# Attention branches: the 512-column score tile ahead of the 384-column one, and POOL scaling it by two per-partition numbers

## The chip, the cores and the metric

The kernel runs on one core of one Trainium2 chip. Its engines are PE (matrix products), DVE (vector operations), ACT (activation functions), POOL (GpSimd) and SP (which here issues DMAs). The metric is the device time of one execution in microseconds. Before the change it is 1286.28 us, the median of 3 runs (1286.25 to 1287.93).

## What is computed

A trunk of two layers on a sequence of 512 tokens, all in float32. Each layer has a mixer of three parallel parts (sparse attention, gated linear attention, spatial gating), an output projection and a feed-forward block. The change touches only the attention's two large branches, selected and window attention:

```python
NSA_HEADS, HEAD_DIM, SEQ, DEPTH = 8, 64, 512, 2
def masked_softmax(s, mask):
    s = where(mask, s, -inf)
    e = exp(s - max(s))
    return e / sum(e)
p = masked_softmax(einsum('bqghd,bgqmd->bghqm', qb, ksel), tok <= t)
o_slc = einsum('bghqm,bgqmd->bqghd', p, vsel)
p = masked_softmax(einsum('bqghd,bkgd->bghqk', qb, kwb), wmask)
o_win = einsum('bghqk,bkgd->bqghd', p, vwb)
return gb[..., 0:1] * o_cmp + gb[..., 1:2] * o_slc + gb[..., 2:3] * o_win
```

With 512 tokens both branches attend to every earlier token, each with keys and values of its own. Their two gates are per token, head and branch.

## The kernel before, in words

The attention stage of a layer (in `mixer`, from line 1188 on) loops over 8 heads, taken in pairs (`hp`, `hh`), and in each head over 2 branches (`br`). A branch works on 4 query tiles `i` of 128 tokens; tile `i` has 128 x (i+1) key columns, so the score tiles are 128, 256, 384 and 512 columns wide. The two narrow ones (`i` below `NBOTH` = 2) are computed for both branches at once when a head starts (lines 1209 to 1225); the other two in the loop at line 1228, the 384-column one first. For each tile PE multiplies queries by keys into a PSUM bank (L1234, L1235: the second product also adds the causal mask), DVE takes the negated row maximum (L1237), and ACT takes the exponential with the row sums as a by-product (L1239; L1222 for the narrow tiles). A row sum is a column of `den`, which is 128 x 4.

When all four sums are there, DVE takes their reciprocals at once (L1244) and multiplies them by the gates of the four tiles (L1245), giving `rr`. Then every tile is scaled in place by its column of `rr`, on three engines (line 1247): tiles 0 and 1 by DVE (L1253), tile 2 by ACT (L1251), tile 3 by POOL (L1249), where the column is handed over as a second tensor broadcast along the row. A dependency added by hand (line 1255) keeps POOL's scaling behind DVE's last one.

Then come the products with the values. For key tiles `j` in the groups `JG` = (0), (1), (2, 3), PE transposes the 128 x 128 blocks of the scaled tiles into a PSUM bank (L1262; group 0 takes tiles 0, 1, 2, 3 in that order), ACT copies the bank into a high part (L299) and DVE takes the low part (L300, both in `split_psum`), and PE multiplies both parts by the values into the head's output bank (L1275, L1276). The compressed branch is added (L1286, L1287), ACT and DVE bring the result out (L1288, L1289).

Score banks form a ring of 3, transpose banks a ring of 2. A scheduler sets the order on each engine's queue from the program order, priorities and costs of its own; at run time each engine takes its queue in order and waits on semaphores. The scheduler puts other work between: products of the output projection (L336 to L338, their weights cast by ACT at L318 and split by DVE at L321, their sums added by DVE at L500), the preparation of queries (L1120, L1125, L1126; L1186 is a copy of them on POOL) and the compressed branch's softmax (`prep_c`, L1140 to L1160).

Of the kernel before, what the change touches and what calls it, by code (L numbers as in the profile page):

```python
# [16 lines left out]
ALU = mybir.AluOpType  # L17
AX = mybir.AxisListType

P = 128  # L20
# [4 lines left out]
NT = SEQ // P  # L25
# [27 lines left out]
NBOTH = 2  # L53
# [90 lines left out]
def trunk_kernel(ctx: ExitStack, tc: tile.TileContext, a, out):  # L144
# [24 lines left out]
    def small(n, tag, bufs=4, dt=F32):  # L169
        return sm.tile([P, n], dt, tag=tag, name=nm(tag), bufs=bufs)  # L170
# [396 lines left out]
    def mixer(l, norm, xkt, eu=None):  # L567
# [65 lines left out]
        with tc.tile_pool(name=f"mx{l}", bufs=1, reuse_waits="tile") as mp:  # L633
# [427 lines left out]
            with tc.tile_pool(name=f"mt{l}", bufs=1, reuse_waits="tile") as tp_:  # L1061
# [126 lines left out]
                for hp in range(H // 2):  # L1188
                    if hp % 2 == 0:
                        okt[hp // 2] = kt_tile()  # L1190
                    kt = okt[hp // 2]
                    oc = tmp()
                    for hh in range(2):
                        h = 2 * hp + hh
                        g, h4 = h // GH, h % GH
                        prep(h, 0)
                        qa = qm1[h % GH]
                        for n in range(h, h + 2) if h < H - 1 else ():
                            if n == 0 or n > h:
                                load_q(n)  # L1200
                        O = psum(OT[h % len(OT)])
                        first = True
                        for br in range(2):
                            if br == 1:
                                prep(h, 2)
                            if br == 0:
                                dens = [small(NT, "den", 4) for _ in range(2)]
                                both = []
                                for i in range(NBOTH):
                                    n = P * (i + 1)  # L1210
                                    S = psum("s")
                                    S3 = S[:, 0 : 2 * n].rearrange("p (b k) -> p b k", b=2)
                                    tk = slice(i * P, (i + 1) * P)
                                    kd = km1[g][:, :, 0:2, :] if i else km1[g][:, :, 6, :]
                                    nc.tensor.matmul(S3, qst[g][:, h4, tk], km2[g][:, :, 0:n], start=True, stop=False)
                                    nc.tensor.matmul(S3, qa[:, tk], kd, start=False, stop=True)
                                    nmx = small(2, "nmx", 8)
                                    nc.vector.tensor_reduce(nmx, S3, axis=AX.X, op=ALU.max, negate=True)
                                    pb = []
                                    for b_ in range(2):  # L1220
                                        p_ = tp_.tile([P, n], F32, tag=f"P{i}", name=nm("P"), bufs=P0B[i])
                                        nc.scalar.activation(p_, S3[:, b_], AF.Exp, bias=nmx[:, b_ : b_ + 1],  # L1222
                                                             accum_out=dens[b_][:, i : i + 1])
                                        pb.append(p_)
                                    both.append(pb)
                            den = dens[br]
                            ps_ = [pb[br] for pb in both]
                            for i in range(NBOTH, NT):
                                n = P * (i + 1)
                                S = psum("s")  # L1230
                                tk = slice(i * P, (i + 1) * P)
                                kd = km1[g][:, br, 0:6, :]
                                kd = kd.rearrange("p (n s) c -> p n s c", s=2)[:, :, 0, :] if i == 2 else kd.rearrange("p (o x) c -> p o x c", o=2)[:, :, 0:3:2, :]
                                nc.tensor.matmul(S[:, 0:n], qst[g][:, h4, tk], km2[g][:, br, 0:n], start=True, stop=False)  # L1234
                                nc.tensor.matmul(S[:, 0:n], qa[:, tk], kd, start=False, stop=True)  # L1235
                                nmx = small(1, "nmx", 8)
                                nc.vector.tensor_reduce(nmx, S[:, 0:n], axis=AX.X, op=ALU.max, negate=True)  # L1237
                                p_ = tp_.tile([P, n], F32, tag=f"P{i}", name=nm("P"), bufs=P0B[i])
                                nc.scalar.activation(p_, S[:, 0:n], AF.Exp, bias=nmx, accum_out=den[:, i : i + 1])  # L1239
                                ps_.append(p_)  # L1240
                            if br == 0:
                                prep(h, 1)
                            rr = small(NT, "rr", 4)
                            nc.vector.reciprocal(rr, den)  # L1244
                            nc.vector.tensor_tensor(rr, rr, gates[:, :, 3 * h + 1 + br], op=ALU.mult)  # L1245
                            scaled = None
                            for i in SORD:
                                if i in ISP:
                                    p3 = nc.gpsimd.tensor_tensor(ps_[i], ps_[i], rr[:, i : i + 1].to_broadcast([P, P * (i + 1)]), op=ALU.mult)  # L1249
                                elif i in ISA:  # L1250
                                    nc.scalar.activation(ps_[i], ps_[i], AF.Copy, scale=rr[:, i : i + 1])  # L1251
                                else:
                                    scaled = nc.vector.tensor_scalar(ps_[i], ps_[i], rr[:, i : i + 1], None, op0=ALU.mult)  # L1253

                            tc.add_manual_dep(p3.ins, scaled.ins.name, mybir.DependencyInfo(mybir.DependencyClass.Sync, mybir.DependencyReason.DATA),
                                              reason="port")
                            for js in JG:
                                T = psum(TT[js[0]])
                                c = 0
                                for j in js:  # L1260
                                    for i in range(j, NT):
                                        nc.tensor.transpose(T[:, c : c + P], ps_[i][:, j * P : (j + 1) * P], ident)  # L1262
                                        c += P
                                if js[0] < JS:
                                    pt = mp.tile([P, 2, c], F32R, tag="PT", name=nm("PT"), bufs=3)
                                    split_psum(pt[:, 0, :], pt[:, 1, :], T[:, 0:c])
                                else:
                                    pf = mp.tile([P, c], F32, tag="PT", name=nm("PT"), bufs=3)
                                    nc.scalar.copy(pf, T[:, 0:c])
                                c = 0  # L1270
                                for j in js:
                                    n = SEQ - j * P
                                    lhs = vst[:, j, br, g].rearrange("p s d -> p (s d)")
                                    if js[0] < JS:
                                        nc.tensor.matmul(O[:, j * P : SEQ], lhs, pt[:, 0, c : c + n], start=first, stop=False)  # L1275
                                        nc.tensor.matmul(O[:, j * P : SEQ], lhs, pt[:, 1, c : c + n], start=False, stop=False)  # L1276
                                    else:
                                        nc.tensor.matmul(O[:, j * P : SEQ], lhs.bitcast(F32), pf[:, c : c + n],
                                                         start=False, stop=False)
                                    first = False  # L1280
                                    c += n
                        prep(h, 3)
                        lhs = vcb[:, g, h4].rearrange("p s d -> p (s d)")
                        hs = slice(64 * hh, 64 * hh + 64)
                        ls = slice(64 - 64 * hh, 128 - 64 * hh)
                        nc.tensor.matmul(O, lhs, pcT[g][0], start=False, stop=False)  # L1286
                        nc.tensor.matmul(O, lhs, pcT[g][1], start=False, stop=True)  # L1287
                        nc.scalar.copy(oc[hs, :], O[ls, :])  # L1288
                        nc.vector.tensor_tensor(oc[hs, :], oc[hs, :], O[hs, :], op=ALU.add)  # L1289
                    split_psum(kt[:, hp % 2, 0, :], kt[:, hp % 2, 1, :], oc)  # L1290
# [416 lines left out]
```

## Time and profile before

| what | value |
|---|---|
| median of 3 runs | 1286.28 us |
| the profiled execution, its own time | 1286.52 us |
| its span in the trace | 1284.7 us |
| outside the span | 1.8 us |
| PE busy | 1257.3 us |
| DVE busy | 918.2 us |
| ACT busy | 677.0 us |
| POOL busy | 160.5 us |
| granted TensorE clock, mean | 0.997 |

The span runs from the first to the last instruction of the trace. In a timeline a row gives the start and duration in us, the engine, the source line, the operation and its tiles (written ones left of the arrow), and in square brackets the idle time just before it and what ended that. Groups give the count, the busy time, the mean in ns of one, and the idle time before them by what ended it. In the view of one line the three numbers behind the count are the shortest, median and longest duration in ns.

### The profile page before, as it was taken

Reading aid. Unit: us, or ns where it says so; the run is one execution under the profiler, and the core shown is the slowest. Engines: PE = TensorE matmul, PEld = TensorE weight load, DVE = VectorE, ACT = ScalarE, POOL = GpSimd, SP = SyncE. Lnnn points to the kernel's source line nnn. Section 1 sums busy time; section 2 is a strip of 40 time slices with the busy share of each in tenths; the row PEclk is TensorE's granted clock in tenths of the full one; section 3 lists DMA queues with packets and bytes.
Section 4 is the critical chain, followed back from the end, with each engine's and each line's share of the span. In section 5 each row is a group of like instructions: output and inputs, shape, how many; then the busy total and the mean of one; then the engine's idle time right before and its main releaser. Section 6 shows DMA issues by size and latency. Waiting matters only on the chain. (4 is left out here: it accounts for less than half of the span.)

```text
span 1284.7 us, 18046 instructions
## 1 busy us (share of the span) xinstructions
PE 1257.3 (98%) x6678; PEld 1038.5 (81%) x6678; DVE 918.2 (71%) x1645; ACT 677.0 (53%) x1288; POOL 160.5 (12%) x157
## 2 busy tenths in 40 slices
PE   8999999999999999999999999999999999999997
PEld 7888788778888888888888877777788888888886
DVE  6767799977856775587446678998767457827775
ACT  6675367864533553354346733788544445515532
POOL 0101222122000100010301012121210001000102
PEclk9999999999999999999999999999999999999999
DMA  6451441034335885483434317210533448754811
GB/s 231 142 180 34 115 108 33 17 87 127 98 105 141 197 232 146 111 200 99 115 94 149 116 34 175 64 33 3 146 98 99 131 117 210 216 130 133 227 66 66
DMA packets 134204, 155.01 MB, mean 121 GB/s; under 512 B 9307, under 2 KB 86885, under 8 KB 134117
## 3 DMA queue, kind: packets, MB, share of 16 engines
q1 hardware_dynamic: 117392, 128.81, 33.3%
q0 software_dynamic: 10208, 20.84, 9.2%
q10 hardware_dynamic: 6516, 4.22, 1.5%
q8 instruction: 52, 0.85, 0.3%
q14 instruction: 36, 0.29, 0.1%
HBM read 149.92 MB, written 2.10 MB: 118 GB/s over the span
## 5 line engine op out<-in xcount | busy, mean ns | idle before, releaser
L318 ACT CAST hl<-raw 128x1024 fp32r<-128x1024 f32 (+3 forms) x170 | 175.2, 1035 | 226.5 <-PE banks L338 160.9
L321 DVE TENSOR_TENSOR hl<-raw,hl 128x1024 fp32r<-128x1024 f32 (+3 forms) x170 | 207.1, 1222 | 94.6 <-ACT hl L318 93.0
L336 PE MATMUL banks<-hl,kt 128*128 128x512 f32 (+2 forms) x688 | 257.9, 375 | 1.1 <-ACT hl L318 1.1
L337 PE MATMUL banks<-hl,kt 128*128 128x512 f32 (+2 forms) x688 | 256.4, 373 | 0.0
L338 PE MATMUL banks<-hl,kt 128*128 128x512 f32 (+2 forms) x688 | 256.1, 373 | 0.0
L337 PE MATMUL banks<-kt,hl 128*128 128x512 f32 x384 | 151.5, 394 | 0.0
L338 PE MATMUL banks<-kt,hl 128*128 128x512 f32 x384 | 151.1, 394 | 0.0
L336 PE MATMUL banks<-kt,hl 128*128 128x512 f32 x384 | 150.4, 394 | 0.0
L336 PEld LDWEIGHTS banks<-hl,kt 128*128 128x128 f32 x688 | 129.5, 188 | 23.6 <-ACT hl L318 1.9
L337 PEld LDWEIGHTS banks<-hl,kt 128*128 128x128 f32 x688 | 129.5, 188 | 21.8 <-DVE hl L321 0.3
L338 PEld LDWEIGHTS banks<-hl,kt 128*128 128x128 f32 x688 | 129.4, 188 | 21.7
L318 ACT CAST hl<-wx 128x1024 fp32r<-128x1024 f32 x48 | 50.5, 1052 | 79.8 <-PE banks L338 69.1
L337 PEld LDWEIGHTS banks<-kt,hl 128*128 128x128 f32 x384 | 72.2, 188 | 14.7 <-DVE kt L295 0.9
L338 PEld LDWEIGHTS banks<-kt,hl 128*128 128x128 f32 x384 | 72.3, 188 | 13.7
L336 PEld LDWEIGHTS banks<-kt,hl 128*128 128x128 f32 x384 | 72.0, 188 | 13.3 <-ACT kt L299 0.3
L321 DVE TENSOR_TENSOR hl<-wx,hl 128x1024 fp32r<-128x1024 f32 x48 | 58.7, 1224 | 18.4 <-ACT hl L318 18.2
L500 DVE TENSOR_TENSOR xT<-xT,banks 128x512 f32<-128x512 f32 x56 | 37.5, 681 | 47.6 <-PE banks L338 47.6
L337 PE MATMUL banks<-act,hl 128*128 128x512 f32 x172 | 67.0, 390 | 0.0
L338 PE MATMUL banks<-act,hl 128*128 128x512 f32 x172 | 66.9, 389 | 0.0
L336 PE MATMUL banks<-act,hl 128*128 128x512 f32 x172 | 66.9, 390 | 0.0
L300 DVE TENSOR_TENSOR PT<-banks,PT 128x384 fp32r<-128x384 f32 (+1 forms) x96 | 54.6, 597 | 14.1 <-ACT PT L299 13.2
L336 PE MATMUL banks<-hl,act 128*128 128x512 f32 (+1 forms) x164 | 63.0, 384 | 0.0
(356 smaller groups left out, 2404.1 us busy)
## 6 DMA issues: line engine op xcount, KB each, us to landing
raw<-in_w_gate_dram SPq DMA_DIRECT2D x44, 512.0 KB, 3.9
raw<-in_w_up_dram SPq DMA_DIRECT2D x44, 512.0 KB, 4.0
raw<-in_w_in_dram SPq DMA_DIRECT2D x32, 512.0 KB, 3.7
raw<-in_w_down_dram SPq DMA_DIRECT2D x36, 256.0 KB, 4.0
raw<-in_w_down_dram SPq DMA_DIRECT2D x18, 512.0 KB, 3.7
raw<-in_w_out_dram SPq DMA_DIRECT2D x16, 512.0 KB, 4.3
raw<-in_cmp_w_k_dram SPq DMA_DIRECT2D x8, 512.0 KB, 3.9
raw<-in_cmp_w_v_dram SPq DMA_DIRECT2D x8, 512.0 KB, 4.9
```

Of the source, the lines that this page charges most:

```text
L300: nc.vector.tensor_tensor(lo, src, hi.bitcast(F32), op=ALU.subtract)
L318: last_cast[:] = [nc.scalar.copy(hl[:, 0, 0:n], raw[:, 0:n])]
L321: e_.tensor_tensor(hl[:, 1, 0:n], raw[:, 0:n], hl[:, 0, 0:n].bitcast(F32), op=ALU.subtract)
L336: nc.tensor.matmul(ps, lh, rh, start=start, stop=False, skip_group_check=skip)
L337: nc.tensor.matmul(ps, lh, rl, start=False, stop=False, skip_group_check=skip)
L338: return nc.tensor.matmul(ps, ll, rh, start=False, stop=stop, skip_group_check=skip)
L500: nc.vector.tensor_tensor(xT[:, m, :], xT[:, m, :], ps, op=ALU.add)
```

## The change

The loop over the two wide tiles runs backwards, so the 512-column tile (`i` = 3) comes before the 384-column one. As soon as the 512-column tile's exponential is there, DVE takes the reciprocal of its one row sum into a new small tile `rc` (L1243 of the changed kernel), and POOL scales the tile by two per-partition numbers, that reciprocal and the gate (L1244). The three other sums are inverted later (L1248), multiplied by their gates (L1249) and used as before (ACT L1255, DVE L1257). The dependency that kept POOL behind DVE is gone. Each of the 32 branches has one DVE instruction more. Lines behind the edit move: the transposes are L1264, the products with the values L1277 and L1278, the scores L1235 and L1236, the maximum L1238, the exponential L1240.

```diff
                             ps_ = [pb[br] for pb in both]
-                            for i in range(NBOTH, NT):
+                            rc = small(NT, "rc", 4)
+                            for i in range(NT - 1, NBOTH - 1, -1):
...
                                 nc.scalar.activation(p_, S[:, 0:n], AF.Exp, bias=nmx, accum_out=den[:, i : i + 1])
-                                ps_.append(p_)
+                                ps_.insert(NBOTH, p_)
+                                if i == NT - 1:
+                                    nc.vector.reciprocal(rc[:, i : i + 1], den[:, i : i + 1])
+                                    nc.gpsimd.tensor_scalar(p_, p_, rc[:, i : i + 1], gates[:, i, 3 * h + 1 + br : 3 * h + 2 + br], op0=ALU.mult, op1=ALU.mult)
                             if br == 0:
                                 prep(h, 1)
                             rr = small(NT, "rr", 4)
-                            nc.vector.reciprocal(rr, den)
-                            nc.vector.tensor_tensor(rr, rr, gates[:, :, 3 * h + 1 + br], op=ALU.mult)
+                            nc.vector.reciprocal(rc[:, 0:3], den[:, 0:3])
+                            nc.vector.tensor_tensor(rr[:, 0:3], rc[:, 0:3], gates[:, 0:3, 3 * h + 1 + br], op=ALU.mult)
                             scaled = None
                             for i in SORD:
                                 if i in ISP:
-                                    p3 = nc.gpsimd.tensor_tensor(ps_[i], ps_[i], rr[:, i : i + 1].to_broadcast([P, P * (i + 1)]), op=ALU.mult)
+                                    continue
...
-                            tc.add_manual_dep(p3.ins, scaled.ins.name, mybir.DependencyInfo(mybir.DependencyClass.Sync, mybir.DependencyReason.DATA),
-                                              reason="port")
```

The scheduler orders the two attention stages anew; outside them the queues keep their order. On DVE, in the first branch of the second head of layer 0, the queue before (`den` holds the row sums, `P` the tiles, `nmx` the maxima, `PT` the low parts of transposed tiles):

```order
L1244 RECIPROCAL rr_2022<-den_1992 128x4
L1237 TENSOR_REDUCE nmx_2058<-banks 128x1
L300 TENSOR_TENSOR PT_1949<-banks,PT_1949 128x512
L300 TENSOR_TENSOR PT_1957<-banks,PT_1957 128x384
L1245 TENSOR_TENSOR rr_2022<-rr_2022,gates_278 128x4
L1237 TENSOR_REDUCE nmx_2064<-banks 128x1
L1253 TENSOR_SCALAR P_1998<-P_1998,rr_2022 128x128
L1253 TENSOR_SCALAR P_2006<-P_2006,rr_2022 128x256
```

And the same branch in the changed kernel:

```order
L1243 RECIPROCAL rc_2014<-den_1996 128x1
L321 TENSOR_TENSOR hl_3066<-raw_3064,hl_3066 128x1024
L300 TENSOR_TENSOR PT_1953<-banks,PT_1953 128x512
L300 TENSOR_TENSOR PT_1961<-banks,PT_1961 128x384
L1248 RECIPROCAL rc_2014<-den_1996 128x3
L1238 TENSOR_REDUCE nmx_2065<-banks 128x1
L1249 TENSOR_TENSOR rr_2029<-rc_2014,gates_278 128x3
L1238 TENSOR_REDUCE nmx_2073<-banks 128x1
L300 TENSOR_TENSOR PT_1969<-banks,PT_1969 128x384
L1257 TENSOR_SCALAR P_2002<-P_2002,rr_2029 128x128
L1257 TENSOR_SCALAR P_2010<-P_2010,rr_2029 128x256
```

The one-column reciprocal, which releases POOL, now stands six rows ahead of the product (L1249) that makes the factors of the other scalings, with a weight split (L321, both operands in SBUF) right behind it.

On PE, where the first branch of layer 0 turns from scores to transposes, the queue before (`hl` are weights of the output projection, `qst` and `qm` queries, `km` keys):

```order
L1234 MATMUL banks<-km_180_1596,qst_1804 128x384
L1235 MATMUL banks<-km_182_1598,qm_184_1600 128x384
L1234 MATMUL banks<-km_180_1596,qst_1804 128x512
L1235 MATMUL banks<-km_182_1598,qm_184_1600 128x512
L336 MATMUL banks<-kt_1591,hl_2898 128x512
L1262 MATMUL banks<-ident,P_1832 128x128
L1262 MATMUL banks<-ident,P_1840 128x128
L1262 MATMUL banks<-ident,P_1848 128x128
```

The transposes of POOL's tile (P_1854) stand three rows further on. And in the changed kernel:

```order
L336 MATMUL banks<-kt_1591,hl_2930 128x512
L1215 MATMUL banks<-km_180_1596,qst_1804 128x256
L1216 MATMUL banks<-km_182_1598,qm_185_1601 128x256
L337 MATMUL banks<-kt_1591,hl_2930 128x512
L338 MATMUL banks<-kt_1591,hl_2930 128x512
L336 MATMUL banks<-kt_1591,hl_2930 128x512
L337 MATMUL banks<-kt_1591,hl_2930 128x512
L338 MATMUL banks<-kt_1591,hl_2930 128x512
L336 MATMUL banks<-kt_680,hl_2930 128x512
L1264 MATMUL banks<-ident,P_1832 128x128
L1215 MATMUL banks<-km_180_1596,qst_1804 128x512
L1264 MATMUL banks<-ident,P_1840 128x128
```

Six products of the output projection and the next head's first scores, which stood behind the first transposes, now stand ahead of them.

## The prediction

> **What bounds the kernel now.** The page comes first. It says which engine is full:
>
> ```profile
> span 1284.7 us, 18046 instructions
> PE 1257.3 (98%) x6678; PEld 1038.5 (81%) x6678; DVE 918.2 (71%) x1645; ACT 677.0 (53%) x1288; POOL 160.5 (12%) x157
> ```
>
> PE is busy 98% of the span, so only places where PE stands still can give time back. The edited lines run in the attention stage alone, from about 176 to 272 us (layer 0) and 807 to 903 us (layer 1). The view by stretches of 10 us (columns: PE, PEld, DVE, ACT, POOL busy us) shows who is full there:
>
> ```profile
> 185.00:195.00 10.00, 9.84 (x53) 7.99 (x52) 9.64 (x23) 8.23 (x24) 1.04 (x1) 1.00 0.01 2
> 225.00:235.00 10.00, 9.15 (x51) 6.81 (x50) 9.91 (x28) 8.21 (x24) 2.08 (x2) 1.00 0.07 21
> 235.00:245.00 10.00, 9.45 (x54) 7.11 (x53) 9.53 (x22) 8.19 (x24) 2.08 (x2) 1.00 0.12 35
> 245.00:255.00 10.00, 9.45 (x54) 7.15 (x53) 7.84 (x21) 9.06 (x27) 2.08 (x2) 1.00 0.00 0
> 255.00:265.00 10.00, 8.75 (x50) 6.64 (x50) 8.95 (x22) 8.39 (x25) 2.08 (x2) 1.00 0.01 2
> 852.00:862.00 10.00, 9.20 (x46) 6.90 (x45) 9.72 (x27) 8.67 (x26) 2.68 (x3) 1.00 0.00 0
> 862.00:872.00 10.00, 9.41 (x57) 7.37 (x56) 9.71 (x23) 8.51 (x24) 1.04 (x1) 1.00 0.19 55
> ```
>
> Three engines are close to full together. PE loses little early, where products of the output projection fill its gaps, and most in the later heads. DVE is at 95% or more while PE has gaps in two stretches of each layer (225 to 245, 852 to 872). Next, the view of the line that is changed, POOL's scaling of the widest tile:
>
> ```profile
> L1249 POOL TENSOR_TENSOR P<-P,rr x32: 1039/1040/1043, 183.3 to 902.0; 128x512 f32<-128x512 f32 x32
>   DVE P L1253: 50.9, 10
> ...
>   PEld banks L1262: 5.3, 12
>   PE banks L1262: 2.3, 8
> ```
>
> It runs 32 times for 1.04 us, often starts when DVE's scaling ends (the 50.9 us of idle POOL cost nothing in themselves), and PE's transposes wait for it: 2.3 us booked on the matmuls, 5.3 us on their weight loads. The timeline of one such place:
>
> ```profile
> 226.44 0.39 PE L336 MATMUL banks<-kt,hl 128*128 128x512 f32 x1
> 226.67 0.40 PE L337 MATMUL banks<-kt,hl 128*128 128x512 f32 x1
> ...
> 227.57 0.17 DVE L1244 RECIPROCAL rr<-den 128x4 f32<-128x4 f32 x1
> ...
> 227.79 1.04 POOL L1249 TENSOR_TENSOR P<-P,rr 128x512 f32<-128x512 f32 x1 [3.19 <-DVE rr L1244]
> ...
> 228.13 0.49 PE L1234 MATMUL banks<-km,qst 128*128 128x512 f32 x1
> 228.23 0.62 DVE L1245 TENSOR_TENSOR rr<-rr,gates 128x4 f32<-128x4 f32 x1
> ...
> 228.89 0.44 PE L1262 MATMUL banks<-ident,P 128*128 128x128 f32 x2 [0.26 <-POOL P L1249]
> ```
>
> A matmul of 512 columns is followed by the next after 0.23 us (226.44 to 226.67). Here 0.76 us pass (228.13 to 228.89), so 0.53 us are lost where 0.26 is booked. The idle time counts from a modelled end and shows about half of the loss.
>
> **The change part by part.** First, POOL's wait. The widest tile is now scored and exponentiated first, its own reciprocal follows at once, and POOL starts without DVE's scalings. What of PE's waits for POOL goes away? At least the booked 2.3 us, at most the 5.3 us of the weight loads (a part of which PE covers by matmuls still streaming). Doubled by the place above, 2.3 becomes 4.6; the middle of the bounds is 3.8. I take 4.0 us for both layers. That the new wait does not come out as late needs rows for what stands between:
>
> ```profile
> L1237 DVE TENSOR_REDUCE nmx<-banks 128x1 f32<-128x512 f32 x16 | 10.9, 681 | 0.0
> L1237 DVE TENSOR_REDUCE nmx<-banks 128x1 f32<-128x384 f32 x16 | 8.8, 547 | 0.8 <-PE banks L1235 0.8
> L1239 ACT ACTIVATE P<-banks,nmx 128x512 f32<-128x512 f32 x16 | 11.2, 700 | 3.0 <-DVE nmx L1237 3.0
> L1239 ACT ACTIVATE P<-banks,nmx 128x384 f32<-128x384 f32 x16 | 9.4, 589 | 2.3 <-PE banks L1262 1.7 <-DVE nmx L1237 0.3 <-DVE PT L300 0.2
> L1239 ACT ACTIVATION_READ_ACCUMULATOR P<-banks,nmx 128x1 f32 x32 | 6.7, 210 | 0.0
> L1244 DVE RECIPROCAL rr<-den x32: 164/174/179, 181.3 to 900.2; 128x4 f32<-128x4 f32 x32
> L1245 DVE TENSOR_TENSOR rr<-rr,gates x32: 93/160/892, 181.9 to 900.4; 128x4 f32<-128x4 f32 x32
> L1245 DVE TENSOR_TENSOR rr<-rr,gates 128x4 f32<-128x4 f32 x32 | 8.6, 268 | 0.3
> L1253 DVE TENSOR_SCALAR P<-P,rr x64: 269/312/355, 182.6 to 901.5; 128x128 f32<-128x128 f32 x32, 128x256 f32<-128x256 f32 x32
> L1186 POOL CAST qm<-qst x12: 602/604/612, 175.1 to 854.4; 64x512 fp32r<-64x512 f32 x12
> L353 POOL TENSOR_TENSOR nacc<-nacc,nsq x21: 1283/1397/1852, 289.0 to 938.8; 128x512 f32<-128x512 f32 x21
> ```
>
> After the widest tile's exponential, ACT still has the 384-column one (0.59 + 0.21 for its sum), then DVE the reciprocal (0.17), the product with the gates (0.16) and two scalings (2 x 0.31): 1.75 us at least, even if nothing stands between. POOL's new instruction with two per-partition scalars isn't in this trace. It reads one wide tile, as the CAST of half the partitions does (0.60 us), and not two, as L353 does (1.40 us); L1249 with its broadcast operand (1.04 us) is nearest, and I take 1.0. All three fit under 1.75 us, so its length costs nothing; beyond 1.75 us each further 0.1 us would cost up to 3.2 us in 32 branches. [...]
>
> Second, DVE. Each branch gets one more reciprocal: 32 x 0.17 = +5.5 us. L1245 is one of two DVE instructions whose operands both lie in SBUF; in the place above it took 0.62 us and ended with POOL's scaling (228.85 and 228.83). Over all 32 it is busy 8.6 us where its median gives 32 x 0.16 = 5.1, so POOL's scaling costs DVE 3.5 us today. With POOL started earlier this is returned where the product stands far enough behind. The order shows that in 20 branches over 1.3 us of other DVE work comes between the one-column reciprocal and the next DVE instruction with two SBUF operands or a scaling. In 8 it follows within 0.8 us, and may be held for 0 to 0.73 us (0.892 less 0.16): 0 to 5.8 us. In 4 more the weight split L321 follows directly:
>
> ```profile
> L321 DVE TENSOR_TENSOR hl<-raw,hl x6: 1215/1222/1752, 169.0 to 231.5; 128x1024 fp32r<-128x1024 f32 x6
> ```
>
> There DVE loses 0 to 0.53 us each (1.752 less 1.222), together 0 to 2.1, or POOL waits 1.2 us, which the 1.75 us hold only in part. DVE's sum: 5.5 - 3.5 + (0 to 7.9) = +2 to +10 us; with something under half of the new holds, +5. How much of that reaches the end? Where DVE is full and PE is not, which is 20 of some 96 us in each layer, about a fifth: +1.0 us. Bounds are 0 and all 10.
>
> Third, edits with one answer. The last tile is now the narrower one, so its reduction and exponential are 0.13 and 0.11 us shorter; in a stage where three engines are nearly full I take nothing for it. The gate multiplication of the widest tile moves into POOL's second scalar, and the product on DVE has three columns, not four: nothing. POOL's queue still holds the query copies (L1186) between scalings; a scaling behind two of them starts up to 1.2 us later. DMA issues keep their order.
>
> Sum against the profiled execution: 1286.52 - 4.0 + 1.0 = 1283.5 us. The median of the runs shown is 0.24 lower (1286.28), so 1283.3 us.
>
> **The rivals.** A measurement here tells a change of about 0.2% (2.6 us) from none: faster means below 1283.7, slower above 1288.9.
>
> *DVE becomes the bound (slower).* The place is the stretch from 245 us on and its twin, where DVE has 1 to 2 us of room in 10. If the holds come at their upper end (+10) and 8 of these 10 us delay the transposed tiles that PE waits for, it is 8 - 4 = +4 us: 1290.3. It decides from a DVE share of 9.5 in 10 in the stretches now at 7.84 and 8.95. The manual wait that the change removes kept POOL's scaling off DVE's, which speaks for it; that 20 of 32 branches have 1.3 us of harmless work between speaks against. [...]
>
> *The wait only changes its name (no change).* ACT's scaling of the 384-column tile already stands idle for the reciprocal's product:
>
> ```profile
> L1251 ACT ACTIVATE P<-P,rr 128x384 f32<-128x384 f32 x32 | 20.0, 624 | 8.3 <-DVE rr L1245 8.3
> ```
>
> That tile is now the last to be exponentiated, and its scaling (0.62 us) the last link before the transposes. If PE then waits for ACT or DVE as long as for POOL, 4.0 come back: 1286.3, give or take 1.5. The same happens if POOL starts no earlier, because the reciprocal stands late in DVE's queue.
>
> *More than the wait goes (faster by more).* PE also waits for the copies of transposed tiles:
>
> ```profile
> L1275 PE MATMUL banks<-PT,vst 128*128 128x512 f32 (+3 forms) x128 | 43.9, 347 | 5.3 <-ACT PT L299 3.2 <-DVE tmp L1289 1.6
> ```
>
> If the full 5.3 us of POOL waits go, and, with transposes grouped earlier, about half of these 3.2: -5.3 - 1.6 = -6.9, 1279.4. Against it: those waits are for ACT's copy, which the change leaves alone.
>
> **How the numbers follow.** The forecast (1281.5 to 1285.0 by itself) gets 0.36: 0.27 of it below 1283.7, 0.09 above. The larger gain gets 0.15, the renamed wait 0.26, the DVE bound 0.23. So faster 0.27 + 0.15 = 0.42, within 0.2% 0.09 + 0.26 = 0.35, slower 0.23. The range 1277.5 to 1290.5 takes in three of the four cases and the DVE case to a little past its middle; outside are about 0.03 below and 0.12 above.
>
> **What would show it.** In the profile after: POOL's scaling as TENSOR_SCALAR of 0.6 to 1.4 us; PE's and PEld's waits for it under 0.5 and 1.5 us together; the product of three columns with a mean of at most 0.25 us; DVE in the stage busier by 2 to 3 us a layer; PE at 9.3 or more in 255 to 265 us. I am wrong if PE still waits for POOL, if L1257 or the product takes 0.8 us in many branches, if waits for ACT's scaling take POOL's place, or if POOL's instruction takes over 1.75 us.

## The result, and the profile after

| | median | runs |
|---|---|---|
| before | 1287.05 us | 6 (1286.25 to 1288.01) |
| after | 1295.08 us | 6 (1294.30 to 1295.74) |
| ratio | 1.0061 | interval 1.0049 to 1.0073 |

The change makes the kernel slower by 8.0 us. The forecast was 1283.3 us with a range of 1277.5 to 1290.5, so both the sign and the range are wrong. The page of the profiled execution (1295.74 us by its own time):

```profile
span 1294.0 us, 18058 instructions
PE 1269.0 (98%) x6678; PEld 1040.9 (80%) x6678; DVE 919.1 (71%) x1677; ACT 677.0 (52%) x1288; POOL 156.2 (12%) x157
```

Against before, PE has as many instructions and 11.7 us more busy time (1257.3), DVE 0.9 us more. In the attention stage itself little is lost. Three of the stretches shown for before, here of the changed kernel (columns: PE, PEld, DVE, ACT, POOL busy us):

```profile
...
245.00:255.00 10.00, 9.63 (x55) 7.17 (x53) 8.33 (x24) 8.17 (x22) 1.55 (x2) 1.00 0.00 1
255.00:265.00 10.00, 9.31 (x50) 6.90 (x50) 8.85 (x23) 8.51 (x26) 1.55 (x2) 1.00 0.01 2
...
862.00:872.00 10.00, 8.59 (x45) 5.89 (x44) 9.18 (x27) 8.39 (x24) 1.55 (x2) 1.00 0.18 52
```

Some stretches of PE are fuller than before (255 to 265: 9.31 for 8.75) and some emptier (862 to 872: 8.59 for 9.41). The views of the changed lines, POOL's scaling, the product of three columns and DVE's scalings (shortest, median, longest in ns, and who waited):

```profile
L1244 POOL TENSOR_SCALAR P<-P,rc,gates x32: 767/776/1602, 182.2 to 906.9; 128x512 f32<-128x512 f32 x32
...
L1249 DVE TENSOR_TENSOR rr<-rc,gates x32: 93/154/276, 184.3 to 907.5; 128x3 f32<-128x3 f32 x32
...
L1257 DVE TENSOR_SCALAR P<-P,rr x64: 266/338/716, 185.6 to 908.0; 128x128 f32<-128x128 f32 x32, 128x256 f32<-128x256 f32 x32
...
  PEld banks L1264: 3.4, 6
  PE banks L1264: 1.6, 4
```

POOL's scaling takes 0.78 us in the median (four of the 32, which run beside a weight split of DVE, L321, take 1.60), and nobody waits for it any more. But PE now waits for DVE's scalings (1.6 us on matmuls, 3.4 us on weight loads), where it waited for POOL (2.3 and 5.3). The place shown in the prediction, in the timeline of the changed kernel:

```profile
227.82 0.78 POOL L1244 TENSOR_SCALAR P<-P,rc,gates 128x512 f32<-128x512 f32 x1 [1.04 <-DVE rc L1243]
...
228.24 0.40 PE L338 MATMUL banks<-kt,hl 128*128 128x512 f32 x1
228.26 0.36 DVE L1158 TENSOR_TENSOR cd<-cd,gates 128x16 f32<-128x16 f32 x1
228.55 0.27 DVE L1257 TENSOR_SCALAR P<-P,rr 128x128 f32<-128x128 f32 x1
228.75 0.68 DVE L1160 TENSOR_TENSOR tmp<-tmp,cd 128x512 f32<-128x512 f32 x1
...
228.88 0.33 PE L1264 MATMUL banks<-ident,P 128*128 128x128 f32 x1 [0.24 <-DVE P L1257]
229.35 0.34 DVE L1257 TENSOR_SCALAR P<-P,rr 128x256 f32<-128x256 f32 x1
...
229.74 0.88 PE L1264 MATMUL banks<-ident,P 128*128 128x128 f32 x6 [0.53 <-DVE P L1257]
...
230.37 0.48 PE L1235 MATMUL banks<-km,qst 128*128 128x512 f32 x1
```

POOL is done at 228.60. DVE's first scaling starts behind a small product of the compressed branch (L1158) that ends just then, 228.62, after 0.36 us (before the change this product takes 0.172 us at most), and a second product (L1160, 0.68 us) stands between the two scalings. PE's transposes wait twice.

None of this makes 8 us. ACT's casts of weights (L318), paired by rank, show where they arise: they lie 1.4 us later than before at 373 us, as they did from the start of the run, 5.5 us later at 642 and 710, and 5.6 us later at 798. The last matmuls, paired from the end, lie 5.8 us later at 915 us, behind the second attention stage, and 9.2 us later at 1273. Both attention stages together cost about nothing; the two feed-forward (FFN) stages cost 4.1 and 3.4 us. There the order on every engine is what it was. What has changed is the time of one matmul, for the operands `act` and `op` (the FFN's activations, and a part of its input) alone. Groups of 512-column matmuls, first before (a PE group names the moving operand and then the stationary one; behind the bar are busy us and mean ns):

```profile
L337 PE MATMUL banks<-hl,kt 128*128 128x512 f32 x560 | 219.1, 391 | 0.0
...
L337 PE MATMUL banks<-act,hl 128*128 128x512 f32 x172 | 67.0, 390 | 0.0
...
L337 PE MATMUL banks<-hl,act 128*128 128x512 f32 x156 | 60.7, 389 | 0.0
...
L337 PE MATMUL banks<-hl,op 128*128 128x512 f32 x64 | 24.9, 389 | 0.0
```

and of the changed kernel:

```profile
L337 PE MATMUL banks<-hl,kt 128*128 128x512 f32 x560 | 219.0, 391 | 0.0
...
L337 PE MATMUL banks<-act,hl 128*128 128x512 f32 x172 | 68.0, 396 | 0.0
...
L337 PE MATMUL banks<-hl,act 128*128 128x512 f32 x156 | 61.6, 395 | 0.0
...
L337 PE MATMUL banks<-hl,op 128*128 128x512 f32 x64 | 25.3, 395 | 0.0
```

These durations (0.39 us) are longer than the steps between starts (0.227 us, below): matmuls overlap here, and what PE loses is read from the steps. A run of such matmuls in the timeline of before, the first and the tenth of ten:

```profile
499.80 0.39 PE L337 MATMUL banks<-act,hl 128*128 128x512 f32 x1
...
501.84 0.39 PE L337 MATMUL banks<-act,hl 128*128 128x512 f32 x1
```

and of the changed kernel, again the first and the tenth:

```profile
504.81 0.40 PE L336 MATMUL banks<-act,hl 128*128 128x512 f32 x1
...
506.91 0.39 PE L336 MATMUL banks<-act,hl 128*128 128x512 f32 x1
```

Nine steps take 2.04 us before (0.2267 each) and 2.10 us after (0.2333 each), without a wait. Three lines each of 172, 156 and 64, and three of 14 with `kt` moving over `act`, are 1218 matmuls; by 0.0066 us that is 8.0 us, as much as was lost. Rows are rounded to 0.01 us, which can make 2.7 us of this product, so it is an estimate; the two FFN stages lost 7.5 us in the trace (4.1 + 3.4).

**The theory.** The new tile `rc` has 4 buffers, each of which takes 32 bytes of a partition. Every tile that is allocated behind it moves up by 128 bytes, `act` and `op` among them, while `hl` and `kt` stay (the first buffer of each; all buffers lie a multiple of 4096 apart, and the group called `op` reads `op7`):

```
tile    start before    start after   (bytes in a partition)
hl          27936           27936
kt          72992           72992
act        130336          130464
op7        163104          163232
```

`act` stood 102400 bytes above `hl`, a multiple of 256; now it stands 128 beyond one. Theory: a 512-column matmul is slower where its two operands don't stand at a multiple of 256 bytes from each other. Rivals: the new schedule itself does it, through traffic that it moves; or the tiles' own place in memory does.

### The profile page after: what moved, and what is told of

It is laid out like the page before. It is cut to its first block, busy times and chain, and to the rows that moved or that the text cites. A ratio compares the mean times of both kernels' runs of the same rounds, so it can differ in the third digit from the quotient of the medians.

```text
span 1294.0 us, 18058 instructions
## 1 busy us (share of the span) xinstructions
PE 1269.0 (98%) x6678; PEld 1040.9 (80%) x6678; DVE 919.1 (71%) x1677; ACT 677.0 (52%) x1288; POOL 156.2 (12%) x157
## 4 chain that ended last, share of the span: by engine, by line
PE 82%; ACT 7%; DVE 6%; DMA 2%; issue 2%; ACTq 0%; DVEq 0%
PE banks L336 22%; PE banks L337 22%; PE banks L338 22%; PE banks L1264 2%; PE banks L1277 2%; DMA raw<-in_w_in_dram 2%; ACT hl L318 1%; PE banks L1278 1%; PE banks L1235 1%; PE banks L471 1%; PE banks L1601 1%; DVE hl L321 1%; PE banks L969 1%; PE banks L1236 1%; ACT PT L299 1%
## 5 line engine op out<-in xcount | busy, mean ns | idle before, releaser
L318 ACT CAST hl<-raw 128x1024 fp32r<-128x1024 f32 (+3 forms) x170 | 175.1, 1034 | 225.6 <-PE banks L338 177.1
L321 DVE TENSOR_TENSOR hl<-raw,hl 128x1024 fp32r<-128x1024 f32 (+3 forms) x170 | 205.9, 1215 | 88.9 <-ACT hl L318 84.3
L318 ACT CAST hl<-wx 128x1024 fp32r<-128x1024 f32 x48 | 50.4, 1049 | 82.6 <-PE banks L338 73.8
L321 DVE TENSOR_TENSOR hl<-wx,hl 128x1024 fp32r<-128x1024 f32 x48 | 58.7, 1223 | 22.3 <-ACT hl L318 21.7
L337 PE MATMUL banks<-act,hl 128*128 128x512 f32 x172 | 68.0, 396 | 0.0
L338 PE MATMUL banks<-act,hl 128*128 128x512 f32 x172 | 67.9, 395 | 0.0
L336 PE MATMUL banks<-act,hl 128*128 128x512 f32 x172 | 67.9, 395 | 0.0
L300 DVE TENSOR_TENSOR PT<-banks,PT 128x384 fp32r<-128x384 f32 (+1 forms) x96 | 55.6, 597 | 14.5 <-ACT PT L299 13.8
L299 ACT CAST PT<-banks 128x384 fp32r<-128x384 f32 (+1 forms) x96 | 47.5, 518 | 33.5 <-PE banks L1264 31.6
```

Source lines behind the costliest of these rows:

```text
L299: nc.scalar.copy(hi, src)
L300: nc.vector.tensor_tensor(lo, src, hi.bitcast(F32), op=ALU.subtract)
L318: last_cast[:] = [nc.scalar.copy(hl[:, 0, 0:n], raw[:, 0:n])]
L321: e_.tensor_tensor(hl[:, 1, 0:n], raw[:, 0:n], hl[:, 0, 0:n].bitcast(F32), op=ALU.subtract)
L336: nc.tensor.matmul(ps, lh, rh, start=start, stop=False, skip_group_check=skip)
L337: nc.tensor.matmul(ps, lh, rl, start=False, stop=False, skip_group_check=skip)
```

## The experiments

The kernel before ran again beside each set of runs; its medians were 1287.03 us (experiments 1 to 3), 1288.08 us (4 to 6) and 1287.63 us (7 and 8). A ratio is to these runs, with its 95% interval.

### 1. The 128 bytes alone

The kernel before, with the tile allocated and never used; the order on every engine is unchanged:

```diff
                             ps_ = [pb[br] for pb in both]
+                            small(NT, "rc", 4)
```

> The kernel before, with four small tiles that nothing uses allocated where the change allocates rc: 128 bytes per partition. Every queue keeps its order, word for word; only the tiles allocated behind move up by 128 bytes. Theory A (place in memory): the loss of the change is these 128 bytes, by which the feed-forward's act and op7 tiles lie otherwise relative to the weight tiles hl; some 1,200 matmuls there take 0.233 us in place of 0.227, so 8 us slower, 1294 to 1296 us. Theory B (schedule): the loss is made in the attention stages by the new order, so this run takes 1286 to 1288 us and its matmuls on act have a mean of 389 ns as before.

Measured: 1295.23 us against 1287.03, ratio 1.0064 (1.0049 to 1.0079). An unused tile costs as much as the whole change. The matmuls with `act` take 395 ns.

### 2. The change without the 128 bytes

The changed kernel, with `rc` as the second half of the tile `rr`, whose 32 bytes have room for it; no tile of the FFN moves, the order is that of the changed kernel:

```diff
-                            rc = small(NT, "rc", 4)
+                            rr = small(2 * NT, "rr", 4)
+                            rc = rr[:, NT : 2 * NT]
...
-                            rr = small(NT, "rr", 4)
```

> The changed kernel with rc put into the unused half of rr's 32-byte slot, so that no tile moves. Every queue has the order of the changed kernel. Theory A: the loss is gone, and what is left is the change itself: 1284 to 1289 us, matmuls on act at a mean of 389 ns. Theory B: 1294 to 1296 us.

Measured: 1287.19 us, ratio 1.0000 (0.9991 to 1.0010). So the edits of the schedule are worth nothing in sum, neither the forecast's -3.0 us nor a loss. The view of DVE's scalings in this run:

```profile
L1257 DVE TENSOR_SCALAR P<-P,rr x64: 268/340/718, 185.5 to 904.7; 128x128 f32<-128x128 f32 x32, 128x256 f32<-128x256 f32 x32
...
  PEld banks L1264: 3.4, 6
  ACT PT L299: 2.9, 2
  PE banks L1264: 1.6, 4
```

As in the changed kernel, PE waits for them and not for POOL.

### 3. All tiles moved, and 256 bytes instead of 128

The kernel before, with 128 bytes ahead of every tile, so that all places change and no distance does:

```diff
+    cp.tile([P, 32], F32, name="front")
     ident = cp.tile([P, P], F32, name="ident")
```

> The kernel before, with 128 unused bytes per partition ahead of the very first tile, so that all tiles, the weight tiles hl and kt with them, move up by 128 bytes and keep their distances. Theory A1 (the place by itself decides): all 512-column matmuls of the kernel are hit, some 4,400 by 6 ns, 20 us slower or more. Theory A2 (the distance between the two operands of a matmul decides): no change, 1286 to 1288 us. Theory B: no change either.

Measured: 1287.64 us, ratio 1.0002 (0.9993 to 1.0012). And the changed kernel with 8 buffers for `rc`, a shift of 256:

```diff
-                            rc = small(NT, "rc", 4)
+                            rc = small(NT, "rc", 8)
```

> The changed kernel with rc in eight buffers and not four, so that the tiles behind move by 256 bytes and not by 128. The order of every queue is that of the changed kernel. Theory A with a period of 256 bytes: matmuls on act back at 389 ns and 1284 to 1289 us. Theory A with a longer period: 395 ns and 1294 to 1296 us, or between. Theory B: 1294 to 1296 us with act matmuls unchanged.

Measured: 1286.81 us, ratio 0.9998 (0.9989 to 1.0008), `act` at 389 to 390 ns. In these two runs it isn't the place that counts but the distance, and a shift of 256 bytes costs nothing.

### 4. A shift of 64 bytes

As in the first experiment, with 2 buffers (`small(NT, "rc", 2)`).

> The kernel before with an unused small tile of 64 bytes in the place where 128 bytes cost 8 us and 256 bytes nothing; the order on every engine is that of before. Theory 'distance': the time of a 512-column matmul hangs on the distance in memory between its two operands, in a pattern that repeats after 256 bytes. If only the middle of the pattern is bad: about 1287 us and 389 ns for the matmuls with act. If it goes up in steps: about 1291 us and 392 ns. If every distance that is no multiple of 256 is bad: about 1295 us and 395 ns. Rival 'a line of 128 bytes': all tiles stood at 32 bytes beyond a multiple of 128 so far, and here those behind the pad stand at 96 for the first time; then other operations than matmuls change their durations too (VectorE and ScalarE on act, PT, P), by some per cent.

Measured: 1292.89 us, ratio 1.0038 (1.0024 to 1.0052), between the cases that were expected. The rival of a 128-byte line falls: DVE's split of `act` (L300) takes 684 ns here and before, ACT's copy of it (L299) 600 and 599 ns. The groups show that the direction counts:

```profile
L336 PE MATMUL banks<-act,hl 128*128 128x512 f32 x172 | 67.4, 393 | 0.0
...
L337 PE MATMUL banks<-hl,act 128*128 128x512 f32 x156 | 61.7, 395 | 0.0
```

With `act` moving, 64 bytes beyond the stationary `hl`, the matmul is slower by less (390 to 393 ns); with `hl` moving, 64 short of `act`, which is 192 beyond a multiple of 256, it has the full 395 ns.

### 5. Matmuls alone

A kernel of nothing but matmuls, in groups of 48 at one distance each (`s` and `m` are where the stationary and the moving operand start):

```diff
+        for i in range(N):
+            nc.tensor.matmul(ps(g, 512), sta(i, s), mov(i, m, 512), start=i == 0, stop=i == N - 1)
```

> A kernel of matmuls alone, with the rest of the computation left out: groups of 48 matmuls of 128x128 by 128x512 (float32r), the stationary operand in steps of 512 bytes and the moving one at a distance from it of 0, 32, 64, 96, 128, 160, 192, 224, 256 and 384 bytes beyond a multiple of 512, each group on a line of its own, all twice; one group with both operands moved up by 128, one with the stationary one alone, two of 256 columns at 0 and 128. No other engine works meanwhile. Theory 'distance': the groups at 0, 256 and with both moved take the same, those at 128 and 384 and with the stationary one alone moved take 2 to 3 per cent more (in the kernel: 389 and 395 ns, one start every 0.227 and 0.233 us). Rival 'traffic': the slowing needs other engines or transfers that write into the same memory meanwhile, and all groups take the same within 1 ns.

The timeline of the second pass, with the groups from 0 (L43) to 256 (L59) in steps of 32, then the stationary operand alone moved by 128 (L61), both moved by 128 (L63), 384 (L65), and the first group of 256 columns (L67). Each row holds 48 matmuls:

```profile
243.49 11.09 PE L43 MATMUL banks<-mem 128*128 128x512 f32 x48
254.42 11.37 PE L45 MATMUL banks<-mem 128*128 128x512 f32 x48
265.62 11.16 PE L47 MATMUL banks<-mem 128*128 128x512 f32 x48
276.62 11.37 PE L49 MATMUL banks<-mem 128*128 128x512 f32 x48
287.83 11.36 PE L51 MATMUL banks<-mem 128*128 128x512 f32 x48
299.03 11.40 PE L53 MATMUL banks<-mem 128*128 128x512 f32 x48
310.27 11.35 PE L55 MATMUL banks<-mem 128*128 128x512 f32 x48
321.46 11.35 PE L57 MATMUL banks<-mem 128*128 128x512 f32 x48
332.65 11.05 PE L59 MATMUL banks<-mem 128*128 128x512 f32 x48
343.54 11.32 PE L61 MATMUL banks<-mem 128*128 128x512 f32 x48
354.70 11.10 PE L63 MATMUL banks<-mem 128*128 128x512 f32 x48
365.63 11.32 PE L65 MATMUL banks<-mem 128*128 128x512 f32 x48
376.79 5.92 PE L67 MATMUL banks<-mem 128*128 128x256 f32 x48
```

From one group's start to the next, divided by 48:

| moving less stationary, mod 256 | us a matmul |
|---|---|
| 0 (L43), 256 (L59), both moved by 128 (L63) | 0.2277, 0.2269, 0.2277 |
| 64 (L47) | 0.2292 |
| 32, 96, 128 (L45, L49, L51) | 0.2333, 0.2335, 0.2333 |
| 160, 192, 224 (L53, L55, L57) | 0.2342, 0.2331, 0.2331 |
| 128 by the stationary one alone (L61), 384 (L65) | 0.2325, 0.2325 |

The kernel gives the other engines nothing to do meanwhile: in the groups at 0 and 64 (243.5 to 254.4 and 265.6 to 276.6 us) DVE, ACT and POOL are busy for 0.00 us, and transfers move 2 and 0 GB/s. So the traffic rival falls. The mean of the first row is 0.2274. The table also prices experiment 4: 516 matmuls with `act` moving stand at 64 and take 0.0018 us more, 702 others stand at 192 and take 0.0057 more. That is 0.9 + 4.0 = 4.9 us, and 4.9 were measured (0.0038 of 1288). For the change itself it gives 1218 x 0.0059 = 7.2 us, where 8.0 were measured in an interval of about 6.3 to 9.4. The two groups of 256 columns, at 0 and at 128, took 5.75 and 5.76 us from start to start in the first pass, so there the distance does nothing.

### 6. The order alone, the scaling alone

Why is the rest of the change worth nothing? Two kernels take it apart, both without a moved tile. The order alone (widest tile first, POOL scales as before):

```diff
-                            for i in range(NBOTH, NT):
+                            for i in range(NT - 1, NBOTH - 1, -1):
...
-                                ps_.append(p_)
+                                ps_.insert(NBOTH, p_)
```

> The kernel before with the widest tile first, and nothing else: POOL scales as before, behind VectorE's scaling, and no tile moves in memory. Theory 'the wait changes its name' (the schedule of the change was worth 0.0 us once its tiles stood still): 1286 to 1288 us; POOL's scaling still starts after the reciprocal of all four sums, the waits for POOL at the transposes stay near 5 us together. Rival 'the order costs and the scaling gains, and the two cancel': 1288.5 to 1291 us.

Measured: 1298.44 us, ratio 1.0080 (1.0066 to 1.0093). Neither theory expected a loss of 10 us. The transposes in this run wait for POOL far more than before (9.2 and 14.8 us, where it was 2.3 and 5.3):

```profile
L1262 PE MATMUL banks<-ident,P 128*128 128x128 f32 x320 | 55.7, 278 | 10.0 <-POOL P L1249 9.2 <-DVE qst L1126 0.5 <-DVE pcT L300 0.3
...
L1262 PEld LDWEIGHTS banks<-ident,P 128*128 128x128 f32 x320 | 38.9, 140 | 22.4 <-POOL P L1249 14.8 <-DVE qst L1126 1.1 <-DVE pcT L300 0.9
```

POOL is hardly later than before: from the end of a branch's last exponential to the end of its scaling it is 4.10 us on average here and 4.05 before. It is PE that comes to the transposes earlier: from a branch's last score product to its first transpose it is 7.50 us on average, with 37.6 matmuls between, where it was 8.16 us and 41.2. What the scheduler moved to bring that about was not taken apart. The scaling alone (the new loop body, over `range(NBOTH, NT)` with `append`, on the kernel of experiment 2, so also without the dependency that held POOL):

> The kernel before with POOL's scaling by two per-partition numbers, with its own reciprocal and at once, and nothing else: the tiles come in the old order (384 columns, then 512), and no tile moves in memory. Theory 'the wait changes its name': 1286 to 1288 us, the waits for POOL fall from about 5 to 1 to 3 us and those for VectorE's scaling go up by as much. Rival 'the order costs and the scaling gains, and the two cancel': 1282.5 to 1285.5 us.

Measured: 1285.19 us, ratio 0.9980 (0.9971 to 0.9989), faster by 1.4 to 3.7 us. Transposes and products with the values (L1277), before these lines L1262 and L1275:

```profile
L1264 PE MATMUL banks<-ident,P 128*128 128x128 f32 x320 | 51.7, 275 | 0.4 <-DVE qst L1126 0.3
...
L1277 PE MATMUL banks<-PT,vst 128*128 128x512 f32 (+3 forms) x128 | 44.2, 348 | 2.6 <-DVE tmp L1291 1.8 <-ACT PT L299 0.8
```

The wait of the transposes' matmuls for POOL is gone, and the one for ACT's copy at the products fell from 3.2 to 0.8; the transposes' weight loads wait 3.3 us for DVE's scalings, where it was 5.3 us for POOL. So the order costs and the scaling gains, as the rival had it: -2.9 us for the scaling, and 0.0 in experiment 2, with the order added. But the two don't add up as it thought. The order costs 10 us with the old scaling and about 3 with the new one.

### 7. What of the order costs

In the run with the scaling alone the factors of the three other tiles (L1249) are ready 0.62 us after a branch's last exponential, in experiment 2 after 1.82 us, and in 12 of 32 branches after more than 2 us, because other DVE work stands ahead in the queue. Here those two instructions get a higher priority:

```diff
+                            with tc.high_priority(offset=60):
-                            nc.vector.reciprocal(rc[:, 0:3], den[:, 0:3])
-                            nc.vector.tensor_tensor(rr[:, 0:3], rc[:, 0:3], gates[:, 0:3, 3 * h + 1 + br], op=ALU.mult)
+                                nc.vector.reciprocal(rc[:, 0:3], den[:, 0:3])
+                                nc.vector.tensor_tensor(rr[:, 0:3], rc[:, 0:3], gates[:, 0:3, 3 * h + 1 + br], op=ALU.mult)
```

> The change without its move of the tiles (rc inside rr's tile), with one thing more: the reciprocal of the three sums and its product with the gates get a higher priority when the queues are laid out, so that VectorE does them soon after a branch's last exp instead of behind other work. Theory 'the old order put these two early, the new order puts them late' (0.6 us after the last exp in the run with the scaling alone, 1.8 us in this schedule, 12 of 32 branches over 2 us): the two come under 1.0 us after the last exp, the waits for VectorE's scaling at the transposes shrink, and the time falls to 1284 to 1286 us. Rival 'what the order costs lies in the score matmuls and exps themselves': the two come early, and the time stays at 1286.5 to 1288.5 us. It can also get worse, since what VectorE did first is now later: 1289 us or more would say that PE waited for that.

Measured: 1287.30 us, ratio 0.9992 (0.9983 to 1.0001). The factors come after 1.15 us, 4 branches over 2 us, and the transposes hardly wait (L1265 here, the products L1278):

```profile
L1265 PE MATMUL banks<-ident,P 128*128 128x128 f32 x320 | 52.7, 273 | 0.2
...
L1278 PE MATMUL banks<-PT,vst 128*128 128x512 f32 (+3 forms) x128 | 45.1, 356 | 3.2 <-ACT PT L299 2.5 <-ACT P L1222 0.5
```

Yet the time does not come down to the 1284 to 1286 us that the theory asked for. The products wait 2.5 us for ACT's copy, where the scaling alone has 0.8. Some factors are still late, and the total times don't tell how much the late ones cost: the ratio's interval takes in 1 and overlaps that of the scaling alone. The traces narrow it. From the start of PE's 901st matmul to that of its 1801st, and from the 2401st to the 1601st counted from the end, PE does the two attention stages and other work whose order no run changes. The two stretches together take, in the one profiled execution of each:

| run | us |
|---|---|
| before; the change without moved tiles (experiment 2) | 324.4; 324.4 |
| order alone | 333.8 |
| scaling alone | 321.9 |
| the change, three factors early (this experiment) | 323.6 |

Runs in which PE has the same order lie within 0.6 us of each other here (324.2 to 324.7 with that of before, 324.4 to 324.9 with that of the change). So the order costs 2.5 us behind the new scaling, and taking a good half of the factors' delay away brings 0.8 us of it back, hardly more than that spread. The rest stays open.

### 8. The other parts

The dependency that held POOL behind DVE, dropped from the kernel before and nothing else (the two lines of `tc.add_manual_dep`):

> The kernel before without the one dependency that holds POOL's scaling behind VectorE's; the two scale different tiles, so nothing else orders them. POOL still multiplies by a broadcast operand, behind the reciprocal of all four sums. Theory 'the gain of the scaling alone comes from its early start': POOL starts about 0.6 us earlier, a third of what its own reciprocal gives, and the time falls by 0 to 1.5 us, 1285.8 to 1287.3 us. Rival 'it comes from the dropped dependency': 1285 us, as with the scaling alone. The two engines can also hold each other, since both scale at the same moment: the scaling of VectorE over 0.35 us, and 1288 us or more.

Measured: 1288.75 us, ratio 1.0004 (0.9995 to 1.0013). The dropped dependency by itself gains nothing (the two stretches of experiment 7 take 326.2 us, 1.8 more than before), so the gain of the scaling alone comes from POOL's early start or its shorter instruction, which no run separates. Where both scale at the same moment, DVE is held by POOL:

```profile
L1253 DVE TENSOR_SCALAR P<-P,rr x64: 273/343/1137, 183.8 to 904.3; 128x128 f32<-128x128 f32 x32, 128x256 f32<-128x256 f32 x32
...
  PEld banks L1260: 4.7, 10
  PE banks L1260: 1.5, 6
```

DVE's scalings last up to 1.14 us (before: 0.355), and PE waits for them as it did for POOL. Of the 64, 17 are held, and each of these ends 0.08 to 0.15 us behind POOL's instruction.

Next, the scaling alone with the attention stage's operands brought to multiples of 256 from each other, by 128 unused bytes behind `gates`:

```diff
             gates = mp.tile([P, NT, 24], F32, name=nm("gates"))
+            mp.tile([P, 32], F32, name=nm("gap"))
```

> The run with the scaling alone (1285.2 us), and an unused tile of 128 bytes behind gates in the attention stage's memory: PT, km2, km1, qr, pcT and P move up by 128 bytes, vst, qst and all tiles of the FFN stay. The matmuls of PT with vst, of km with qst and of pcT with vcb then stand at a multiple of 256 from each other, where they stood at 128 beyond one. Theory 'distance, felt only where matmuls follow each other without a wait': 1284 to 1285.5 us, and the 512-column matmuls of those groups take up to 6 ns less. Rival 'the distance works in every matmul': about 300 matmuls by 6 ns is 1.8 us at most, 1283.4 us. Either way the FFN's matmuls stay at 389 ns, and the run repeats the gain of the scaling alone.

Measured: 1285.32 us, ratio 0.9981 (0.9972 to 0.9990). The products of 512 columns with the values keep their 470 ns (L1277) and 433 (L1278; now 432); nothing is gained, and the gain of the scaling alone repeats. At last the changed kernel with 128 bytes more, ahead of the FFN's tiles alone:

```diff
         with tc.tile_pool(name=f"ff{l}", bufs=1, reuse_waits="tile") as fp:
+            fp.tile([P, 32], F32, name=nm("gap"))
```

> The changed kernel as it is, and an unused tile of 128 bytes ahead of the FFN's tiles: act, op7 and the others of the FFN stand 256 bytes above where they stood before, the tiles of the attention stages 128 bytes as in the changed kernel. Theory 'all of the loss is the distance of act and op7 from hl': 1286 to 1288 us, act at 389 ns. Rival 'the attention stages' tiles lose a part': 1288.5 to 1293 us.

Measured: 1287.90 us, ratio 1.0003 (0.9994 to 1.0012), `act` at 389 to 390 ns. The loss is the FFN's alone, within that interval.

## Why the prediction was wrong

**The step that failed** is the third part, "edits with one answer". It went through what the edits do and never through what the new tile `rc` does to memory: 128 bytes ahead of `act` and `op`. That is the missing term of the sum, +8.0 us. The prediction's opening shuts it out: only places where PE stands still were to matter, as if the time of a matmul were fixed, and here PE's busy time rose by 11.7 us with the same instructions. The unused tile of experiment 1 shows it alone. The change without it is shown three times: with no tile moved (experiment 2), with the moved tiles shifted by 256 (experiment 3) and with the FFN's tiles alone brought to 256 (experiment 8). Experiment 5 shows it in matmuls with nothing else running. No wait and no queue tells of it; PE's busy time and the means of untouched groups do.

**POOL's wait, -4.0 us.** That POOL's scaling starts early and nobody waits for it was right. That the 4.0 us come back was wrong: at the place that was used to size them (0.53 us lost for POOL) the changed kernel loses 0.41 and 0.75 us for DVE's scalings, start to start as in the prediction (228.24 to 228.88 less 0.23; 228.88 to 229.74 less 0.11, the step of the six transposes from 229.74 to 230.37). Ahead of them in DVE's queue stand L1158 and L1160, which the prediction leaves out where it counts DVE's instructions with both operands in SBUF. The rival "the wait only changes its name" describes the schedule's share, 1286.3 us give or take 1.5, against a ratio of 1.0000 in experiment 2. It named ACT's scaling as the last link and let PE wait for ACT or DVE; it was DVE's scalings (L1257).

**The length of POOL's instruction.** Taken as 1.0 us from the rows of before (0.60, 1.04 and 1.40), measured 0.776 in the median. As foreseen, the length cost nothing: nobody waits for it.

**DVE, +5 us busy, +1.0 to the end.** DVE has 0.9 us more in all. The long holds of the product are gone (longest 0.276 us, before 0.892), while two of the 64 scalings are held to 0.716 us (before, none took over 0.355), which the prediction saw only as a possibility. Of its two outcomes for the weight splits that follow the one-column reciprocal, it was POOL that waited (four scalings of 1.60 us). The rival "DVE becomes the bound" does not hold: in 245 to 255 us its share is 8.33 of 10, not 9.5. The forecast's "PE at 9.3 in 255 to 265" came true and meant nothing for the end.

**One edit that was costed at nothing has a price.** The order of the tiles and the scaling were taken as one step. Apart, the scaling is worth -2.9 us, and the order takes that back; with the old scaling it costs 10 us. That -2.9 lies close to the forecast's sum of -3.0 is luck: the sum was for both edits together, and its +1.0 for DVE did not come. The prediction looked at which link is last in a branch, and not at what other work the new order leaves in front of the transposes.

The best version measured is the scaling alone without a moved tile, 1285.2 us, 0.2% under before and 0.8% under the changed kernel.

## What to carry to other kernels

A new tile moves every tile allocated behind it, here by 128 bytes: compare the operands' addresses before and after an edit, and look at the mean duration of groups that the edit does not touch, before you explain a difference by waits. A wait that is taken away is worth only what the next link leaves, so price that link first. Split a change into its parts: here a gain and a loss of 3 us hid in a sum of nothing.

## What was not expected of the hardware

In experiment 5 a 128x512 float32r matmul starts every 0.227 us where the moving operand stands at a multiple of 256 bytes from the stationary one, every 0.229 us at 64 beyond, and every 0.2325 to 0.234 us at the other distances that were timed (steps of 32 bytes), 2 to 3% more. The pattern goes by the distance (both moved: 0.2277), needs no other engine, and does not show at 256 columns (5.75 and 5.76 us for 48, at 0 and 128). In the attention stage it did not show either: with the same operands 128 beyond a multiple of 256 or at one, the first products with the values (512 columns) took 470 ns, in runs of few matmuls with waits between. Why the distance matters no run here shows.
